# Stick-breaking queries and keys: one whole copy out of PSUM on ScalarE, then hi and lo from SBUF

## The chip, the cores and the metric

The kernel runs on one core of a Trainium2 chip. The metric is device time in microseconds (us): the median of three runs of the kernel before is 1643.02 us (1641.83 to 1644.89). The engines are called as in the profile: PE (TensorE matmul), PEld (TensorE weight load), DVE (VectorE), ACT (ScalarE), POOL (GpSimd), SP (SyncE).

## The reference, cut to what matters

The reference runs three transformer layers (a convolution mixer, a pooling mixer, and a block with two attention branches and a feed-forward part) on 512 tokens of width 1024. The change lies in the third, in stick-breaking attention with 16 heads of width 64:

```python
z = jnp.einsum('bhtd,bhsd->bhts', qb, kb).astype(jnp.float32) * scale      # scale = 64 ** -0.5 = 0.125
log_1m_beta = jnp.where(mask, jax.nn.log_sigmoid(-z), 0.0)
after = lax.cumsum(log_1m_beta, axis=3, reverse=True) - log_1m_beta
log_a = jax.nn.log_sigmoid(z) + after
a = jnp.where(mask, jnp.exp(log_a), 0.0)
outs.append(jnp.einsum('bhts,bhsd->bhtd', a.astype(v.dtype), vb))
```

q, k and v come from one projection of the normed input. Nothing of the mathematics is changed.

## The kernel before, in words

Matmuls run on fp32r numbers. To keep fp32 precision every operand is held as hi (the value rounded to fp32r) and lo (the value less hi), and a product is three matmuls, hi*hi, hi*lo and lo*hi. Weights arrive as fp32 blocks of 128x1024; `group_steps` makes their hi on ACT (L304) and their lo on DVE (L309).

Activations are kept transposed: 128 features on the partitions, 512 tokens in the free dimension. One 128x512 result of a q or k projection (`lin_in`, lines L320 to L322 with the three products) therefore holds two heads, one in partitions 0 to 63 and one in 64 to 127 (`HALF`). It is made in an accumulator `m`, of which there are two in PSUM (`psm`, bufs=2). All of these share the two `m` accumulators in turn: the q and k projections, the v projection (L1037 to L1039), and the output of a head (`sb_out`, L1185). A new user of an accumulator waits until the last reader of the one before has finished.

For a query pair i, `sb_q` makes two tiles of 128x512, one a head: one half holds hi and the other half lo of the same 64 rows. ACT writes the two hi halves from PSUM (L1084, with the factor 0.125), and one tick later DVE writes the two lo halves, reading PSUM again and hi from SBUF (L1087). For a key pair `sb_k` does the like: hi by ACT (L1094), lo by DVE into separate zeroed tiles (L1097), and a second copy of hi into the other half by ACT (L1099).

The stage walks over 16 heads. For head `hd` the steps are W (`sb_weights`: matmuls of the cumulative sums into the score banks z, L1161 and L1164; then ACT takes their exponentials, L1170), O (`sb_out` of the head before, L1185), S (`sb_scores` of the head after next, L1126 to L1134, into z banks that the exponentials just read), and three F (`fill`: half a q or k projection or one block of a v projection, taken in the order of `SB_ORDER`). S also posts the softplus of its scores: a minimum on DVE (L1141), Exp and Ln on ACT (L1142, L1143), a maximum on DVE (L1146), sums on POOL (L1150), hi on DVE (L1109) or ACT (L1107) and lo on POOL (L1110). Work on ACT, DVE and POOL is posted as tasks, and `tick` after each step lets a task go on when its delay of `WAIT` steps is over. The stage is scheduled by hand: each of the engines PE, ACT, DVE and POOL runs its instructions in the order in which the program writes them.

Four heads take two q, two k and one v projection, so the pattern repeats every four heads. Such a stretch is called a round below: the second one goes from about 558 to 617 us. The tag "s" is a ring of 14 buffers of 128x512 that score, softplus and weight tiles of the stage use in turn.

Of the kernel before, what the change touches and what calls it, by code (L numbers as in the profile page):

```python
# [12 lines left out]
ALU = mybir.AluOpType  # L13
# [123 lines left out]
def body(ctx: ExitStack, tc, ap, out):  # L137
# [12 lines left out]
    def nm(p):  # L150
        uid[0] += 1
        return f"{p}{uid[0]}"
# [18 lines left out]
    def at(tag="a", dt=F32, n=T):  # L171
        return phase[0].pool[tag].tile([P, n], dt, tag=tag, name=nm(tag))
# [16 lines left out]
    def f(x):  # L189
        return x.bitcast(F32)  # L190

    mm = nc.tensor.matmul
    V, A, G = nc.vector, nc.scalar, nc.gpsimd
# [8 lines left out]
    with tc.high_priority(offset=20000):  # L202
        for k in range(KC // 2):
            t = const.tile([P, 2 * T], F32, name=nm("x"))
# [124 lines left out]
    def acc():  # L329
        turn[0] += 1  # L330
        return pm() if turn[0] % 2 else pz()
# [491 lines left out]
    with tc.manual_schedule(engines=HAND):  # L823
# [8 lines left out]
        for k in range(KC):  # L832
            t = at("c")
# [36 lines left out]
        raw, zs = {}, [None] * KC  # L870
# [37 lines left out]
    for i in range(4):  # L908
        t = at("v" if i < 2 else "p")
# [117 lines left out]
    def sb_lin(w):  # L1027
        i = int(w[1:])
        if w[0] == "v":

            v_[i] = [at("a", F32R) for _ in range(4)]
            for j in range(4):
                o = pm()
                for k in range(KC):
                    wh, wl = block(2 * k, 2)
                    hh, hl = cols(h[k], j * P, j * P + P)
                    mm(o[:, 0:2 * P], hh, wh, start=k == 0, stop=False)  # L1037
                    mm(o[:, 0:2 * P], hh, wl, start=False, stop=False)
                    mm(o[:, 0:2 * P], hl, wh, start=False, stop=k == KC - 1)  # L1039
                post(split_steps(o[:, 0:2 * P].rearrange("p (h d) -> p h d", h=4), v_[i][j].rearrange("p (h s d) -> p h s d", h=4, s=2)))  # L1040
                if j == 3:
                    at_block[0] += 2 * KC
                yield
            return
        o = yield from lin_in((SBQ if w[0] == "q" else SBK) + i)
        ready[w] = post((sb_q if w[0] == "q" else sb_k)(i, o))
        yield
# [32 lines left out]
    def sb_q(i, o):  # L1080

        q_[i] = [at("a", F32R) for _ in HALF]
        for t, a in zip(q_[i], HALF):
            A.mul(out=t[a], in_=o[a], mul=0.125)  # L1084
        yield WAIT["q"]
        for t, a, b in zip(q_[i], HALF, HALF[::-1]):
            V.scalar_tensor_tensor(out=t[b], in0=o[a], scalar=0.125, in1=f(t[a]), op0=ALU.mult, op1=ALU.subtract)  # L1087

    def sb_k(i, o):

        res, los = [at("a", F32R) for _ in HALF], klo[i % 3]
        k_[i] = res, los
        for t, a in zip(res, HALF):
            A.copy(out=t[a], in_=o[a])  # L1094
        yield WAIT["k"]
        for t, lo, a in zip(res, los, HALF):
            V.tensor_sub(out=lo[a], in0=o[a], in1=f(t[a]))  # L1097
        for t, a, b in zip(res, HALF, HALF[::-1]):
            A.copy(out=t[b], in_=f(t[a]))  # L1099

# [120 lines left out]
    def fill_all():  # L1221
        for w, o in zip(SB_ORDER, first):
            finish(post((sb_q if w[0] == "q" else sb_k)(int(w[1:]), o)))
        for w in SB_ORDER[len(first):]:
            yield from sb_lin(w)
        yield from ret_qk(0)
        for e in range(4):
            o = yield from lin_in(RG + e)
            gate0.append(at("g"))
            V.tensor_copy(out=gate0[-1], in_=o)  # L1230
            yield
# [232 lines left out]
    with tc.manual_schedule(engines=HAND):  # L1464
# [5 lines left out]
        for a in (0, T // 2):  # L1470
            b = a + T // 2
            o = acc()
# [99 lines left out]
```

## Time and profile before

| what | value |
| --- | --- |
| median of three runs | 1643.02 us |
| the profiled execution | 1643.24 us, its span 1641.5 us |
| PE, PEld | 97%, 82% busy |
| DVE, ACT, POOL | 60%, 38%, 33% busy |
| attention stage, 455 to 710 us: PE, DVE, ACT, POOL | 243.9, 182.4, 157.8, 170.1 us busy of 255 |
| granted TensorE clock in that stage | 1.00 |

The profile is of one execution; its time is 1.7 us above its span, which goes from the first instruction to the last. Busy time of PE includes modelled ends of matmuls, so a wait of PE is best read from the waits and from starts in the order of time. A wait is written as idle time before an instruction, with the instruction that ended it.

### The profile page before, as it was taken

The page shows a single profiled execution, that of the slowest core. Times are in us where ns is not written, and L with a number is a line of the kernel's source. Part 1 is how long each engine was busy: PE and PEld are TensorE (multiplying, and loading weights), DVE is VectorE, ACT ScalarE, POOL GpSimd, SP SyncE. Part 2 cuts the span into 40 slices and gives each one's busy share as a digit, 9 for nine tenths or more (in the row PEclk, how much of TensorE's full clock was granted, in tenths as well). Part 3 has the DMA queues.
Part 4 walks back from the last instruction along what each step waited for, and adds up shares of the span by engine and source line. Part 5 has one row for each costly group of instructions (what it writes and reads, how often), then busy time and mean ns, then how long its engine had stood idle before and what let it go on. Part 6 is the DMA issues. An engine that isn't in the chain of part 4 may idle for free.

```text
span 1641.5 us, 20357 instructions
## 1 busy us (share of the span) xinstructions
PE 1584.5 (97%) x7910; PEld 1338.7 (82%) x7910; DVE 986.2 (60%) x1374; ACT 617.1 (38%) x918; POOL 541.4 (33%) x414
## 2 busy tenths in 40 slices
PE   7999899999999999999999999999999999999997
PEld 5788778877887888878878888888888888888887
DVE  7899988797777676874665744433255433333222
ACT  4634434433467656522323222123234322222221
POOL 2567853671256676720210202004522000000001
PEclk8999999999999999999999999999999999999998
DMA  9565444455422111245374321322222232223231
GB/s 347 172 214 184 143 141 148 149 175 196 161 63 67 52 52 52 78 147 165 105 235 144 109 90 54 120 78 90 93 95 75 97 103 93 100 95 99 91 101 52
DMA packets 61059, 197.97 MB, mean 121 GB/s; under 512 B 6689, under 2 KB 8993, under 8 KB 60962
## 3 DMA queue, kind: packets, MB, share of 16 engines
q1 hardware_dynamic: 58978, 193.52, 35.6%
q10 hardware_dynamic: 1984, 3.15, 0.6%
q8 instruction: 62, 1.02, 0.3%
q14 instruction: 35, 0.29, 0.1%
HBM read 194.54 MB, written 2.10 MB: 120 GB/s over the span
## 4 chain that ended last, share of the span: by engine, by line
PE 77%; DVE 10%; ACT 5%; issue 3%; DMA 2%; POOL 2%; SPq 0%; POOLq 0%; DVEq 0%; ACTq 0%
PE m L320 10%; PE m L322 10%; PE m L321 10%; PE z L322 8%; PE z L320 8%; PE z L321 8%; DVE wlo L309 3%; DVE gw L265 1%; DMA gw<-in_wmod 1%; PE m L1293 1%; PE z L1293 1%; PE z L1292 1%; PE m L1292 1%; PE m L1291 1%; PE z L1291 1%
## 5 line engine op out<-in xcount | busy, mean ns | idle before, releaser
L309 DVE TENSOR_TENSOR wlo<-w,whi 128x1024 fp32r<-128x1024 f32 (+1 forms) x244 | 334.0, 1372 | 359.3 <-ACT whi L304 358.8
L304 ACT CAST whi<-w 128x1024 fp32r<-128x1024 f32 x244 | 255.6, 1051 | 591.0 <-PE m L321 254.2
L320 PE MATMUL m<-h,whi 128*128 128x512 f32 x730 | 286.3, 392 | 2.5 <-DVE c L677 1.3
L321 PE MATMUL m<-h,whi 128*128 128x512 f32 x730 | 284.6, 390 | 2.0 <-POOL h L556 2.0
L322 PE MATMUL m<-h,wlo 128*128 128x512 f32 x730 | 285.1, 391 | 1.2 <-DVE wlo L309 1.2
L320 PEld LDWEIGHTS m<-h,whi 128*128 128x128 f32 x730 | 137.2, 188 | 31.3 <-DVE a L1087 1.7
L322 PEld LDWEIGHTS m<-h,wlo 128*128 128x128 f32 x730 | 137.1, 188 | 31.0 <-DVE wlo L309 2.0
L321 PEld LDWEIGHTS m<-h,whi 128*128 128x128 f32 x730 | 137.3, 188 | 29.9 <-POOL h L556 2.3
L410 POOL TENSOR_TENSOR c<-c,c 128x512 f32<-128x512 f32 x10 | 13.4, 1339 | 370.3 <-ACT c L448 370.1
L322 PE MATMUL z<-h,wlo 128*128 128x512 f32 x338 | 132.0, 391 | 0.2 <-DVE e L918 0.2
L320 PE MATMUL z<-h,whi 128*128 128x512 f32 x338 | 132.1, 391 | 0.0
L321 PE MATMUL z<-h,whi 128*128 128x512 f32 x338 | 131.8, 390 | 0.0
L410 POOL TENSOR_TENSOR s<-s,s 128x512 f32<-128x512 f32 x14 | 18.7, 1337 | 321.0 <-ACT s L1331 292.2
L1110 POOL TENSOR_TENSOR s<-s,s 128x512 fp32r<-128x512 f32 x64 | 96.1, 1514 | 12.7 <-DVE s L1109 12.7
L265 DVE CUSTOM_DVE_ANT_0 gw<-gw,cb,vec 128x1024 f32<-128x1024 f32 x59 | 90.1, 1535 | 5.0 <-DMA gw<-in_wmod 4.9
L322 PE MATMUL z<-a,wlo 128*128 128x512 f32 (+1 forms) x222 | 81.8, 368 | 1.5 <-DVE wlo L309 1.5
L320 PE MATMUL z<-a,whi 128*128 128x512 f32 (+1 forms) x222 | 82.1, 370 | 0.0
L321 PE MATMUL z<-a,whi 128*128 128x512 f32 (+1 forms) x222 | 81.5, 367 | 0.0
L322 PEld LDWEIGHTS z<-h,wlo 128*128 128x128 f32 x338 | 63.7, 188 | 14.3 <-DVE e L918 0.6
L321 PEld LDWEIGHTS z<-h,whi 128*128 128x128 f32 x338 | 63.7, 188 | 13.0
L320 PEld LDWEIGHTS z<-h,whi 128*128 128x128 f32 x338 | 63.7, 189 | 12.9
L320 PE MATMUL m<-a,whi 128*128 128x512 f32 (+1 forms) x196 | 71.5, 365 | 0.0
(430 smaller groups left out, 3527.7 us busy)
## 6 DMA issues: line engine op xcount, KB each, us to landing
w<-in_weights SPq DMA_DIRECT2D x244, 512.0 KB, 3.7
gw<-in_wmod SPq DMA_DIRECT2D x86, 512.0 KB, 4.3
a<-in_diag SPq DMA_DIRECT2D x40, 256.0 KB, 5.2
dg<-in_wmod SPq DMA_DIRECT2D x10, 256.0 KB, 7.0
y<-in_wmod SPq DMA_DIRECT2D x10, 256.0 KB, 5.8
x<-in_xt SPq DMA_DIRECT2D x4, 512.0 KB, 6.0
s<-in_dec ACTq DMA_DIRECT2D x4, 256.0 KB, 3.3
out_x<-h SPq DMA_DIRECT2D x4, 256.0 KB, 2.5
```

Of the source, the lines that this page charges most:

```text
L265: product = V.tensor_tensor_reduce(out=t, in0=t, in1=cb[-1][:, a:b], scale=1.0, scalar=mod[:, j:j + 1] if a else bias_of(j), op0=ALU.mult, ...
L304: A.copy(out=hi, in_=w)
L309: e.tensor_tensor(out=lo[:, part], in0=w[:, part], in1=f(hi[:, part]), op=ALU.subtract)
L320: mm(o, l[0], r[0], start=first, stop=False)
L321: mm(o, l[0], r[1], start=False, stop=False)
L322: mm(o, l[1], r[0], start=False, stop=last)
L410: self.eng.tensor_tensor(out=n, in0=self.acc, in1=t, op=ALU.add)
L1110: G.tensor_tensor(out=lo[:, 0:w], in0=t[:, 0:w], in1=f(hi[:, 0:w]), op=ALU.subtract)
L1291: mm(o, hh, wh, start=k == 0, stop=False)
L1292: mm(o, hh, wl, start=False, stop=False)
L1293: mm(o, hl, wh, start=False, stop=k == KC - 1)
```

## The change

`sb_q` and `sb_k` take one new tile each from the ring "s". ACT writes the whole 128x512 accumulator into it in one operation (with the factor for q, a copy for k). The hi halves are then made by ACT from this tile, and the lo halves by DVE, which subtracts hi from it; for q the DVE operation is a plain subtraction now. PSUM is read by the first operation alone.

```diff
     def sb_q(i, o):
 
         q_[i] = [at("a", F32R) for _ in HALF]
+        raw = at("s")
+        A.mul(out=raw, in_=o, mul=0.125)
         for t, a in zip(q_[i], HALF):
-            A.mul(out=t[a], in_=o[a], mul=0.125)
+            A.copy(out=t[a], in_=raw[a])
         yield WAIT["q"]
         for t, a, b in zip(q_[i], HALF, HALF[::-1]):
-            V.scalar_tensor_tensor(out=t[b], in0=o[a], scalar=0.125, in1=f(t[a]), op0=ALU.mult, op1=ALU.subtract)
+            V.tensor_sub(out=t[b], in0=raw[a], in1=f(t[a]))
 
     def sb_k(i, o):
 
         res, los = [at("a", F32R) for _ in HALF], klo[i % 3]
         k_[i] = res, los
+        raw = at("s")
+        A.copy(out=raw, in_=o)
         for t, a in zip(res, HALF):
-            A.copy(out=t[a], in_=o[a])
+            A.copy(out=t[a], in_=raw[a])
         yield WAIT["k"]
         for t, lo, a in zip(res, los, HALF):
-            V.tensor_sub(out=lo[a], in0=o[a], in1=f(t[a]))
+            V.tensor_sub(out=lo[a], in0=raw[a], in1=f(t[a]))
         for t, a, b in zip(res, HALF, HALF[::-1]):
             A.copy(out=t[b], in_=f(t[a]))
```

The new line numbers are L1084 and L1086 (q on ACT), L1089 (q on DVE), L1096, L1098 and L1103 (k on ACT), L1101 (k on DVE); every line behind them is four higher than before (L1174 for L1170, L1189 for L1185).

On ACT, before, the second key of the second round (accumulator m_5543), the weights' hi, one v block and the exponentials of the head whose z banks the next scores take:

```order
L1094 CAST a_5583<-m_5543 64x512
L1094 CAST a_5584<-m_5543 64x512
L1099 CAST a_5583<-a_5583 64x512
L1099 CAST a_5584<-a_5584 64x512
L304 CAST whi_5604<-w_5544 128x1024
L1076 CAST a_5597<-m_5601 128x4x64
L1170 ACTIVATE s_5646<-z_5368 128x512
L1170 ACTIVATE u_5647<-r_5369 128x256
L1170 ACTIVATE s_5648<-z_5370 128x512
```

The same place of ACT after the change:

```order
L1096 COPY s_5607<-m_5565 128x512
L1098 CAST a_5605<-s_5607 64x512
L1098 CAST a_5606<-s_5607 64x512
L1103 CAST a_5605<-a_5605 64x512
L1103 CAST a_5606<-a_5606 64x512
L304 CAST whi_5628<-w_5566 128x1024
L1076 CAST a_5621<-m_5625 128x4x64
L1174 ACTIVATE s_5670<-z_5386 128x512
L1174 ACTIVATE u_5671<-r_5387 128x256
L1174 ACTIVATE s_5672<-z_5388 128x512
```

One row is new, ahead of the two hi casts, which read it; nothing else has moved, and the exponentials stand behind all of it.

On DVE, before, the second query of the second round (accumulator m_5430), between the maxima and the casts of the softplus:

```order
L1146 TENSOR_TENSOR s_5384<-z_5370,s_5384 128x512
L1087 SCALAR_TENSOR_TENSOR a_5467<-m_5430,a_5467 64x512
L1087 SCALAR_TENSOR_TENSOR a_5468<-m_5430,a_5468 64x512
L1109 CAST u_5491<-u_5383 128x256
L1109 CAST s_5495<-s_5382 128x512
```

The same place of DVE after the change:

```order
L1150 TENSOR_TENSOR s_5402<-z_5388,s_5402 128x512
L1089 TENSOR_TENSOR a_5487<-s_5489,a_5487 64x512
L1089 TENSOR_TENSOR a_5488<-s_5489,a_5488 64x512
L1113 CAST u_5513<-u_5401 128x256
L1113 CAST s_5517<-s_5400 128x512
```

The count and the order of DVE's instructions stay; the two of the query read s_5489 and hi, both in SBUF, where they read the accumulator and hi. PE's order does not change.

## Rows read from the trace of the kernel before

**Rows 1.** Waits of PE, 455 to 710 us: total us, times, longest.
```profile
PE m L1185 <- DVE g L1097: 5.0, 3, 1.7
PE m L1185 <- DVE a L1087: 3.5, 3, 1.5
```

**Rows 2.** Busy us (instructions) by stretch: PE, PEld, DVE, ACT, POOL; clock, DMA.
```profile
562.54:569.33 6.79, 6.79 (x33) 5.71 (x32) 1.38 (x2) 6.61 (x11) 2.74 (x3) 1.00 0.00 0
569.36:580.05 10.69, 10.26 (x54) 8.50 (x53) 10.49 (x14) 5.01 (x9) 7.44 (x7) 1.00 0.17 52
580.08:588.30 8.22, 6.36 (x42) 5.52 (x41) 5.69 (x10) 8.02 (x15) 4.56 (x6) 1.00 0.19 64
675.00:710.00 35.00, 35.00 (x174) 29.84 (x173) 28.52 (x39) 16.09 (x29) 26.23 (x21) 1.00 0.20 69
```

**Rows 3.** ACT in order of time, second round: start, us, instruction, idle before.
```profile
562.54 1.18 ACT L1094 CAST a<-m 64x512 fp32r<-64x512 f32 x2 [3.02 <-PE m L322]
...
569.36 1.20 ACT L1084 ACTIVATE a<-m 64x512 fp32r<-64x512 f32 x2
...
580.08 0.63 ACT L1142 ACTIVATE s<-s 128x512 f32<-128x512 f32 x1 [5.63 <-DVE s L1141]
...
583.23 1.17 ACT L1094 CAST a<-m 64x512 fp32r<-64x512 f32 x2
584.31 1.25 ACT L1099 CAST a<-a 64x512 fp32r<-64x512 f32 x2
...
587.68 0.62 ACT L1170 ACTIVATE s<-z 128x512 f32<-128x512 f32 x1
```

**Rows 4.** DVE in order of time, second round.
```profile
569.36 1.23 DVE L309 TENSOR_TENSOR wlo<-w,whi 128x1024 fp32r<-128x1024 f32 x1 [4.22 <-ACT whi L304]
...
572.27 1.39 DVE L1087 SCALAR_TENSOR_TENSOR a<-m,a 64x512 fp32r<-64x512 f32 x2
...
577.02 2.31 DVE L309 TENSOR_TENSOR wlo<-w,whi 128x1024 fp32r<-128x1024 f32 x1
...
589.54 0.74 DVE L1109 CAST s<-s 128x512 fp32r<-128x512 f32 x2
```

**Rows 5.** PE in order of time, second round.
```profile
583.96 0.34 PE L1164 MATMUL z<-s,cstr 128*128 128x384 f32 x1
585.97 1.05 PE L1185 MATMUL m<-s,a 128*128 128x512 f32 x4 [1.67 <-DVE g L1097]
...
588.35 0.50 PE L1126 MATMUL z<-a,a 128*128 128x512 f32 x1
```

**Rows 6.** ACT by line and shape, whole span: count, busy us, mean ns, idle before.
```profile
L1351 ACT COPY a<-m 128x512 f32<-128x512 f32 x4 | 2.3, 576 | 0.0
```

**Rows 7.** PE in order of time, first query of the second round.
```profile
556.60 1.06 PE L1185 MATMUL m<-s,a 128*128 128x512 f32 x4 [1.48 <-DVE a L1087]
...
558.37 0.39 PE L1126 MATMUL z<-a,a 128*128 128x512 f32 x1
```

**Rows 8.** ACT in order of time, the same place.
```profile
553.85 1.18 ACT L1084 ACTIVATE a<-m 64x512 fp32r<-64x512 f32 x2
...
556.88 0.61 ACT L1170 ACTIVATE s<-z 128x512 f32<-128x512 f32 x1
```

**Rows 9.** DVE in order of time, start of the stage.
```profile
475.92 0.42 DVE L1078 TENSOR_TENSOR a<-m,a 128x256 fp32r<-128x256 f32 x1
```

**Rows 10.** PE in order of time, start of the stage.
```profile
476.91 0.28 PE L1037 MATMUL m<-whi,h 128*128 128x256 f32 x1
```

**Rows 11.** POOL in order of time, second round.
```profile
542.05 1.29 POOL L1110 TENSOR_TENSOR s<-s,s 128x512 fp32r<-128x512 f32 x1
...
572.32 0.74 POOL L1150 TENSOR_TENSOR s<-s,u 128x256 f32<-128x256 f32 x1
...
576.90 3.57 POOL L1110 TENSOR_TENSOR s<-s,s 128x512 fp32r<-128x512 f32 x2 [0.43 <-DVE s L1109]
...
589.44 2.00 POOL L1110 TENSOR_TENSOR s<-s,s 128x512 fp32r<-128x512 f32 x1
```

**Rows 12.** DVE by line and shape, 455 to 715 us.
```profile
L393 DVE TENSOR_TENSOR a<-s,a 128x512 fp32r<-128x512 f32 x4 | 2.8, 693 | 0.1
```

## The prediction

> **What bounds the kernel now.** Read the waits of PE in the attention stage first [rows 1]. The reader is to see that PE, busy nearly all the time, waits six times for an accumulator `m` that DVE has not yet finished reading, 5.0 us behind L1097 and 3.5 us behind L1087: 8.5 us in all, and the change frees `m` much sooner, after one ACT operation. That is the gain on offer. It is not yet a gain in time: the question is what PE would wait for next.
>
> So read PE around one of these waits [rows 5]. The last L1164 of step W starts at 583.96 and O (L1185) follows at 585.97, after 1.67 us for DVE's L1097. Then comes S, whose last score matmul (L1126) starts at 588.35. ACT's last exponential of the z bank that it overwrites runs from 587.68 to 588.30 [rows 3]. PE followed it by 0.05 us. The wait for `m` thus ended just before another one: behind it stands ACT.
>
> Now follow ACT and DVE back from 588.30. ACT started this run of work at 580.08, released by DVE's L1141 after 5.63 us idle [rows 3], and was busy 8.02 of the 8.22 us since [rows 2]. DVE started its run at 569.36, released by ACT's weight cast L304 after 4.22 us idle [rows 4], and was busy 10.49 of 10.69 us until L1141's end at 580.05 [rows 2]. ACT started that run at 562.54 with the key cast L1094, released by PE after 3.02 us idle [rows 3], and was busy 6.61 of 6.79 us until the weight cast's end at 569.33 [rows 2]. (The missing 0.2 us in each are the steps from one instruction to the next.) From 562.54 to 588.35 there is one unbroken chain, ACT, DVE, ACT, and then PE. It holds both keys of the round: L1094 at 562.54 and at 583.23 [rows 3]. A share of busy time would not show it: ACT is at 38% over the span.
>
> **The change part by part.**
>
> ACT, added: one 128x512 operation from PSUM for each of 8 queries and 8 keys. A copy of this form takes 0.58 us [rows 6], an activation from PSUM 0.61 [rows 8]. The hi casts can't start before it has ended; a hand-over between dependent instructions is 0.03 us here (DVE's L1141 ends at 580.05, ACT starts at 580.08) [rows 2, 3]. The two hi casts stay, with an SBUF source: two such casts take 1.25 us (L1099) [rows 3]. For a key: 0.58 + 0.03 + 1.25 = 1.86 us in place of 1.18 [rows 3], +0.68. For a query: 0.61 + 0.03 + 1.25 = 1.89 in place of 1.20 [rows 3], +0.69; I count 0.68 for both, and only those on the chain.
>
> Round: two keys on it, 2 x 0.68 = +1.36 us for S at 588.35. The second query's casts (569.36) [rows 3] stand behind the weight cast from which DVE goes on, so they are not on it. The 1.67 us for `m` go: the copy would end at 583.23 + 0.68 + 0.58 = 584.49, and PE comes to O later than before by what has already been lost. O comes early, and PE waits at S for the exponentials. There are three rounds: +4.08 us.
>
> First query of each round: PE's O waited 1.48 us for L1087, until 556.60, and S's last matmul came at 558.37 [rows 7]. ACT's last exponential ended at 556.88 + 0.61 = 557.49 [rows 8]. It ends 0.68 later now, at 558.17, PE follows at 558.22, so of the wait removed only 0.15 us is kept. Three times: -0.45 us.
>
> Start of the stage: query 0 and key 0 are cast one behind the other ahead of the weight casts, and key 1 stands on the same way to the first v blocks: 3 x 0.68 = 2.04 us on the way to DVE's L1078, which ends at 476.34 [rows 9] and frees the accumulator that PE takes at 476.91 [rows 10]. Of it 0.57 us is slack: +1.47 us.
>
> DVE: the 32 lo subtractions. From PSUM and SBUF two take 1.39 us, 0.69 each [rows 4]; a subtraction with both inputs in SBUF takes 0.69 us where it runs alone [rows 12]. So the operation costs the same, and a gain is excluded by that row. But the place of its inputs counts: the weights' lo (L309, both inputs in SBUF) takes 1.23 us at 569.36 and 2.31 at 577.02 [rows 4], where POOL's L1110 had begun at 576.90; there two L1110 take 3.57 us [rows 11], where one alone takes 1.29 [rows 11]. Each waited for the other. It can fall to DVE too: at 589.54 two casts take 0.74 us [rows 4] and it is POOL's L1110 of 589.44 that takes 2.00 [rows 11]. The second query's pair (572.27) is on the chain, with POOL's L1150 of 0.74 us beginning at 572.32 [rows 11]. Its cost is between 0 (DVE keeps its turn) and 0.74 us (the second subtraction waits for the whole L1150). The two rows speak for one end each, so I take the middle, 0.35 to 0.37, say 0.35 us a round: +1.05 us. The keys' pairs lie beside ACT's work: DVE has 4.22 us idle after the first [rows 4].
>
> The Trainium skill says on this, in "SBUF — State Buffer", section "Who interferes with whom", that a VectorE instruction with two SBUF inputs contends with a GpSimd one that reads SBUF, and that whichever issues second is blocked until the first is done. The trace agrees with the blocking (2.31 against 1.23 us). By that rule L1150 issues ahead of the second subtraction and the term would be 3 x 0.74 = 2.2 us in place of 1.05, the time 1650.3.
>
> Ring "s": the new tile waits for POOL in most cases. For the first query of the second round the built program gives it the buffer that POOL's L1110 of 542.05 read last, free at 543.34 [rows 11]; the cast stands at 553.85 [rows 8]. Cost nothing, hidden by 10 us. No DMA is added or moved.
>
> Sum: 4.08 - 0.45 + 1.47 + 1.05 = 6.15 us, on the profiled execution's 1643.24 us (span 1641.5 and 1.7 us around it) 1649.4; the median of runs stands 0.2 us below, so **1649.2 us**. Nothing gives it back after the last key: from 675 to 710 us PE is busy 35.00 of 35.00 us [rows 2], and what follows starts from PE.
>
> **The rivals.**
>
> Faster: the accumulator waits are what counts, and PE is through O and S earlier. All 8.5 us of rows 1 go: 1643.0 - 8.5 = 1634.5. For it: PE is the engine that is busy, and these waits are its longest. Against it: the exponential that ends 0.05 us ahead of the last score matmul. It decides if the chain through ACT has slack of 0.68 us or more between key and exponential; its busy shares leave 0.2.
>
> No change: DVE's chain catches up. L309 at 577.02 lost 2.31 - 1.23 = 1.08 us to POOL; if DVE comes later and meets a free POOL, a round gets 1.08 back: 6.15 - 3.24 = 2.9, 1645.9. Against it: that L1110 was released by DVE's own L1109 (0.43 us idle before it) [rows 11], so it moves along.
>
> Slower still: every subtraction of the second query waits for POOL, once 0.74 (L1150) and once 1.29 us (L1110), 2.03 a round in place of 0.35: 6.15 + 5.04 = 11.2, 1654.2. It decides if POOL has an instruction under way when each subtraction is issued. POOL is busy 7.44 of 10.69 us there [rows 2], but only the L1150 are close by.
>
> **How the numbers follow.** What a measurement can tell from no change here is about 0.2%, 3.3 us. The forecast has 0.58, with its own range 1648 to 1651 (the middle term at 0 gives 1648.1, at 0.74 1650.3, and 0.05 us on each of nine tasks 0.5 more). No change has 0.14, faster 0.07, slower still 0.21. Faster by over 0.2%: 0.07; within: 0.14; slower: 0.58 + 0.21 = 0.79. The range goes from 1645.0, which takes in the catching-up case at 1645.9, to 1653.0, where POOL costs most of its bound; left out are the faster case and the far end of the slower one, about 2 in 10.
>
> **What would show it.** In the profile after, PE waits for `m` behind DVE's subtractions should be gone, and L1130 (S) should wait for ACT's L1174 by 1 to 3 us a head in three of four heads, some 15 us in all (the 8.5 of the waits that go and the 6.15 lost). The key's three ACT operations should take 1.86 us, with the exponentials still ending 0.05 us before S. L1089 should read 0.69 us alone and up to 1.4 us beside L1154 on POOL. The prediction is wrong if ACT shows idle time between L1096 and L1174, or if S waits no more than before.

## The result, and the profile after

The changed kernel takes 1653.37 us (median of 4 runs, 1652.64 to 1653.78), the kernel before 1643.42 us in the same comparison; the ratio is 1.006 with a 95% interval of 1.0048 to 1.0072. It is 9.95 us slower. The forecast was +6.15 us, and its range ended at 1653.0. The profiled run took 1652.64 us, its span is 1650.9 us.

The waits of PE in the stage first, with the same columns as [rows 1]:

```profile
PE z L1130 <- ACT s L1174: 11.9, 9, 1.8
PE m L1037 <- DVE a L1078: 0.8, 1, 0.8
```

The 8.5 us behind DVE's subtractions are gone, and in their place stands S (L1130), waiting for the last exponentials of ACT nine times, at three heads of four. So far this is the forecast, though the sum is 11.9 us where it had some 15. The new thing is in the next view, the three rounds by stretch (busy us and instructions of PE, PEld, DVE, ACT, POOL, then the granted clock):

```profile
500.00:558.00 58.00, 54.61 (x303) 48.20 (x302) 38.58 (x60) 36.63 (x69) 39.51 (x35) 0.94 0.16 55
558.00:617.00 59.00, 54.61 (x303) 48.39 (x303) 40.23 (x60) 37.56 (x69) 40.00 (x35) 0.94 0.14 46
617.00:676.00 59.00, 54.60 (x305) 48.45 (x304) 39.34 (x60) 39.84 (x74) 38.39 (x35) 0.94 0.17 54
```

The clock is 0.94; before it was 1.00 in every stretch of [rows 2] and over the whole second round:

```profile
558.00:617.00 59.00, 55.17 (x322) 48.46 (x322) 40.64 (x63) 38.45 (x72) 39.79 (x37) 1.00 0.16 54
```

Cut finer in the second round of the changed kernel, after two of the waits at S:

```profile
576.00:578.00 2.00, 1.59 (x8) 1.35 (x9) 1.94 (x4) 1.95 (x6) 1.69 (x2) 0.92 0.76 256
578.00:580.00 2.00, 2.00 (x7) 1.71 (x7) 1.94 (x4) 1.53 (x3) 1.73 (x2) 0.50 0.05 14
...
594.00:596.00 2.00, 1.91 (x10) 1.68 (x9) 1.95 (x6) 1.64 (x4) 1.44 (x2) 0.68 0.50 129
596.00:598.00 2.00, 2.00 (x10) 1.90 (x10) 1.74 (x4) 0.00 (x0) 2.00 (x2) 0.50 0.33 133
598.00:600.00 2.00, 2.00 (x19) 2.00 (x17) 0.00 (x0) 0.00 (x0) 2.00 (x3) 0.96 0.00 0
```

At 0.50 the clock is at its lower level, 1.2 GHz: from 596 to 598 us PE is busy all the time and does 10 matmuls, where it does 19, nearly all of the same size, in the next 2 us. This happens six times in the stage, twice a round, each time behind the wait at the second or the third S of the round, and each time 1.7 us of clock are lost (the sum of one less the granted clock over short stretches). The Trainium skill says in "TensorE: Matmul & The Clock Gate", section "What's actually happening", that the array's clock follows how busy PE has been and has two levels; the rows agree with that much.

Now PE in order of time, second round: the last score matmul of each S (128x512), and around the third S the end of O and the wait:

```profile
562.11 0.50 PE L1130 MATMUL z<-a,a 128*128 128x512 f32 x1
...
577.09 0.50 PE L1130 MATMUL z<-a,a 128*128 128x512 f32 x1
...
591.37 0.33 PE L1189 MATMUL m<-s,a 128*128 128x128 f32 x2
593.52 0.51 PE L1130 MATMUL z<-a,a 128*128 128x384 f32 x2 [1.81 <-ACT s L1174]
...
594.28 0.50 PE L1130 MATMUL z<-a,a 128*128 128x512 f32 x1
...
609.41 0.39 PE L1130 MATMUL z<-a,a 128*128 128x512 f32 x1
...
623.94 0.51 PE L1130 MATMUL z<-a,a 128*128 128x512 f32 x1
```

From one S to the next this gives four intervals, A to D, in each round: 577.09 - 562.11 = 14.98, then 17.19, 15.13 and 14.53 us. The S at 577.09 is called the second S of the round below, and the one at 594.28 the third. The kernel before starts the same matmuls at 558.37 [rows 7], 588.35 [rows 5] and

```profile
572.00 0.50 PE L1126 MATMUL z<-a,a 128*128 128x512 f32 x1
...
601.96 0.39 PE L1126 MATMUL z<-a,a 128*128 128x512 f32 x1
...
616.75 0.39 PE L1126 MATMUL z<-a,a 128*128 128x512 f32 x1
```

which gives 13.63, 16.35, 13.61, 14.79. A round is 3.45 us longer: A +1.35, B +0.84, C +1.52, D -0.26. The forecast for a round was 1.36 + 0.35 - 0.15 = 1.56, all of it in A, B and D. A and B are read together, since A also holds the copy of the second query, which stands ahead of the exponentials of the second S, and B gives that back (in e11 below, where the pair does not meet POOL, A is 14.84 and B 16.35 as before): +2.19 where 1.71 was forecast. C is new: the matmuls that run at half the clock from 594 on are in it.

ACT in the same place, answering to [rows 3]:

```profile
585.32 0.63 ACT L1146 ACTIVATE s<-s 128x512 f32<-128x512 f32 x1 [5.79 <-DVE s L1145]
...
588.46 0.58 ACT L1096 COPY s<-m 128x512 f32<-128x512 f32 x1
589.07 1.27 ACT L1098 CAST a<-s 64x512 fp32r<-64x512 f32 x2
590.36 1.26 ACT L1103 CAST a<-a 64x512 fp32r<-64x512 f32 x2
591.65 1.04 ACT L304 CAST whi<-w 128x1024 fp32r<-128x1024 f32 x1
...
593.62 0.61 ACT L1174 ACTIVATE s<-z 128x512 f32<-128x512 f32 x1
```

The key takes 588.46 to 590.34, 1.88 us (forecast 1.86). The last exponential ends at 594.23, and PE follows at 594.28, again 0.05 us later. And DVE, where the second query's pair meets POOL:

```profile
576.68 1.83 DVE L1089 TENSOR_TENSOR a<-s,a 64x512 fp32r<-64x512 f32 x2
578.54 1.00 DVE L1113 CAST u<-u 128x256 fp32r<-128x256 f32 x1
```

```profile
576.73 1.23 POOL L1154 TENSOR_TENSOR s<-s,u 128x256 f32<-128x256 f32 x1
578.04 1.35 POOL L1154 TENSOR_TENSOR s<-s,s 128x384 f32<-128x384 f32 x1
```

The pair takes 1.83 us, where the pair from PSUM took 1.39 [rows 4]; and POOL's L1154, which took 0.74 us [rows 11], takes 1.23. Both got longer at once. The Trainium skill says in "SBUF — State Buffer", section "Who interferes with whom", that a VectorE instruction with two SBUF inputs contends with a GpSimd one that reads SBUF; these rows agree.

### The profile page after: what moved, and what is told of

Same layout as the page of the kernel before. It is cut to its first block, busy times and chain, and to the rows that moved or that the text cites. A ratio compares the mean times of both kernels' runs of the same rounds, so it can differ in the third digit from the quotient of the medians.

```text
span 1650.9 us, 20374 instructions
## 1 busy us (share of the span) xinstructions
PE 1590.7 (96%) x7910; PEld 1344.0 (81%) x7910; DVE 991.4 (60%) x1374; ACT 626.5 (38%) x934; POOL 548.9 (33%) x414
## 4 chain that ended last, share of the span: by engine, by line
PE 79%; DVE 9%; ACT 5%; issue 2%; DMA 2%; POOL 1%; SPq 0%; POOLq 0%; DVEq 0%; ACTq 0%
PE m L320 11%; PE m L322 11%; PE m L321 11%; PE z L322 8%; PE z L320 8%; PE z L321 8%; DVE wlo L309 3%; DVE gw L265 1%; DMA dg<-in_wmod 1%; ACT whi L304 1%; PE m L1297 1%; PE z L1295 1%; PE m L1295 1%; PE z L1297 1%; PE m L1037 1%
## 5 line engine op out<-in xcount | busy, mean ns | idle before, releaser
L309 DVE TENSOR_TENSOR wlo<-w,whi 128x1024 fp32r<-128x1024 f32 (+1 forms) x244 | 334.3, 1373 | 359.3 <-ACT whi L304 358.8
```

Source lines behind the costliest of these rows:

```text
L309: e.tensor_tensor(out=lo[:, part], in0=w[:, part], in1=f(hi[:, part]), op=ALU.subtract)
```

## The experiments

Theory A: ACT's part of the chain costs 1:1 and moves PE's idle time to one place, S; the clock falls behind it, and that is what the forecast lacked. Theory B: the fallen clock fills time in which PE would wait anyway, and DVE and POOL are in each other's way more than forecast. All times are medians of 5 runs (e6, e8 and e10 of 11) against the kernel before on the same chip (1643.5, 1642.9 and 1643.0 us in the three comparisons; the changed kernel was measured against 1643.4). In brackets stand the ratio to the kernel before and its 95% interval. The intervals below are those of the second round, from starts of the last score matmul of S in the profiled run; the last column says how many of the three C intervals of the stage had a fallen clock.

| kernel | median us | A | B | C | D | C at half clock |
| --- | --- | --- | --- | --- | --- | --- |
| before | 1643.0 | 13.63 | 16.35 | 13.61 | 14.79 | 0 of 3 |
| changed | 1653.4 | 14.98 | 17.19 | 15.13 | 14.53 | 3 |
| e1 filler, second and third S | 1652.3 | 14.96 | 17.18 | 15.11 | 14.52 | 3 |
| e2 queries only | 1650.0 | 14.36 | 16.50 | 13.62 | 14.51 | 2 |
| e3 keys only | 1649.1 | 14.19 | 17.01 | 15.10 | 14.75 | 2 |
| e4 lo from PSUM | 1649.4 | 14.84 | 16.62 | 16.01 | 14.77 | 1 |
| e5 filler, third S | 1649.0 | 14.97 | 17.21 | 13.59 | 14.49 | 0 |
| e6 copies on DVE | 1644.1 | 13.59 | 15.90 | 13.62 | 14.54 | 2 |
| e7 before, copies on DVE | 1635.3 | 13.03 | 14.88 | 13.50 | 14.77 | 0 |
| e8 keys only, copies on DVE | 1641.2 | 13.07 | 15.51 | 15.11 | 14.78 | 3 |
| e9 before, extra ACT copy | 1649.5 | 14.19 | 16.93 | 14.95 | 14.75 | 1 |
| e10 as e6, filler at third S | 1640.5 | 13.55 | 15.91 | 13.64 | 14.47 | 0 |
| e11 query's lo from PSUM | 1650.6 | 14.84 | 16.35 | 15.04 | 14.77 | 2 |

### Filling the wait: e1 and e5

```diff
         o = pm()
+        for _ in range(4 if hd in (1, 2, 5, 6, 9, 10) else 0):
+            mm(o, v_[i // 2][0][:, hd % 4 * P:hd % 4 * P + P], aa[0][0], start=True, stop=True)
         for j in range(4):
```

> The changed kernel, and on PE four more 128x512 matmuls ahead of O (into the accumulator that O then starts anew) in the six heads whose S waited 1.5 to 2.0 us for ACT; they take about 0.9 us out of that wait and add nothing that is used. Theory A (the idle stretch at S lets the granted clock fall to half for some 3.4 us, and the slow matmuls behind it are what the prediction lacked): clock 1.00 over the stage, S's waits there down to 0.6 to 1.2 us, time 1649 to 1650.5. Theory B (the fallen clock fills time that PE would wait anyway; what was lacking is DVE and POOL in each other's way): the same time as the changed kernel, 1653.4, or up to 1 us more.

Measured 1652.3 us (1.0058, 1.0046 to 1.0071). The wait at the second S fell and the clock stayed there; the third S kept its wait and its fall:

```profile
PE z L1130 <- ACT s L1174: 9.8, 9, 2.0
```

Half of the expectation failed: three falls went, and the time hardly moved. The table says why. B is 17.18 us with the fall (changed) and without it (e1): behind the second S the slow matmuls only use up the wait that PE meets at the third S. C has no such wait at its end, and there the fall goes with 1.5 us. So the next run fills the third S alone.

```diff
+        for _ in range(12 if hd in (2, 6, 10) else 0):
+            mm(o, v_[i // 2][0][:, hd % 4 * P:hd % 4 * P + P], aa[0][0], start=True, stop=True)
```

> As the filler run, but twelve unused matmuls ahead of O in the three heads (at 527, 586 and 644 us of the kernel before) behind whose S PE lost 1.5 us each time that the clock fell, and none elsewhere; the wait at S there falls from 2.2 to about 0.5 us. Theory A' (a fallen clock costs time only where PE is not made to wait for ACT a head later; the three falls behind the other S are hidden by the next wait): these three falls go, the other three stay, and the time is 1653.4 - 3 x 1.5 = 1648.9. Theory B (the falls cost nothing; the loss is in the chain of ACT, DVE and POOL alone): 1652.3 to 1653.4.

Measured 1649.0 us (1.0038, 1.0024 to 1.0052), as theory A' has it. Its second and third rounds:

```profile
558.00:617.00 59.00, 56.02 (x322) 49.09 (x321) 41.32 (x62) 39.15 (x73) 40.08 (x35) 1.00 0.17 54
617.00:676.00 59.00, 55.98 (x324) 49.25 (x323) 41.41 (x61) 39.19 (x72) 41.76 (x36) 1.00 0.19 60
```

C is back at 13.59, A and B of this round are those of the changed kernel. Matmuls that compute nothing of use made the kernel 4.4 us faster than the changed one by the medians; in the profiled runs the three rounds, from the S of 500 us on, are 4.3 us shorter (166.58 against 170.85). (One fall was left, behind the second S of the first round, where the expectation had three. There B is 17.62 and not 17.2: with the wait at the third S filled, such a fall is no longer hidden whole.) Theory B falls in so far as it has the falls cost nothing; that DVE and POOL cost more than forecast is taken up with e4 and e11.

### One part alone: e2 and e3

Kernel e2 has the new `sb_q` and the old `sb_k`, e3 the other way round.

> Only the queries take the new tile; the keys are as before. Theory A: the three waits for m behind L1087 go (3.5 us), those behind L1097 stay (5.0 us); the second query's subtractions cost 0.70 us a round against POOL, the first query gives back 0.45 us in all, the start costs 0.1 us: 2.1 - 0.45 + 0.1 = +1.8, 1645.2, clock 1.00 in the stage. Theory B (contention is the larger part of the loss, about 2 us a round): 1649. If the ring or the order mattered apart from that: above 1649.

> Only the keys take the new tile; the queries are as before. Theory A: ACT's chain is 0.68 us longer for each of six keys, 4.1 us, and 0.8 us at the start: 1648.3 with the clock at 1.00; S waits for ACT at the same places, so the clock falls at some of them and the time is 1650 to 1652. Theory B (contention of the queries' subtractions is the larger part): 1647 to 1648.5, whatever the clock does.

The queries alone: 1650.0 us (1.0042, 1.0028 to 1.0056), 4.8 us over the expectation. Without a fallen clock the second round has A + B + C + D = 58.99, 0.61 over before. But PE's waits for `m` behind the key's subtractions have grown:

```profile
PE m L1187 <- DVE g L1099: 7.0, 3, 2.3
```

They were 5.0 us, 1.7 at most [rows 1]: the contention of the query's pair makes DVE late, the wait at O is longer, and behind it the clock fell in the first and the third round (in the third C is 16.05 us). In the second round the same wait (2.35 us) was not followed by a fall. So this run too has a part of clock that the expectation lacked. The keys alone: 1649.1 us (1.0034, 1.0020 to 1.0048), 0.9 us under the range that theory A gave with a falling clock; C is 15.12 and 15.10 where it fell and 13.60 where it did not. A + B is 31.20, +1.22 for the two keys where the forecast had 1.36.

### Contention: e4 and e11

```diff
-            V.tensor_sub(out=t[b], in0=raw[a], in1=f(t[a]))
+            V.scalar_tensor_tensor(out=t[b], in0=o[a], scalar=0.125, in1=f(t[a]), op0=ALU.mult, op1=ALU.subtract)
```

This is e11; e4 has besides `in0=o[a]` in the key's subtraction.

> ACT as in the changed kernel (whole copy, casts from it), but DVE's subtractions read the accumulator again, as before. This gives up the early release of m and takes away every conflict of these subtractions with POOL. Theory A: the waits for m come back, each 0.7 us later than in the kernel before, so that the idle time is split between O and S and the clock stays at 1.00; 4.1 (keys) + 1.5 (start) + 2.0 (first query of three rounds) = +7.6, 1650.6. Theory B (contention is the larger part of the loss): 1648 or less, since that is gone.

> The changed kernel, but the queries' subtractions read the accumulator and not the new tile (three operations on ACT as in the changed kernel). Theory A: the second query's pair and the cast behind it no longer meet POOL, which gives 0.70 us a round between the S of 558 and of 588 us (a shift of 1.4 us in place of 2.2 there); the waits for m behind L1087 come back and cost 0.25 to 0.7 us a round at the first query; the clock falls as in the changed kernel: 1651.5 to 1653. If contention cost nothing: a shift of 2.2 us there as before, and 1654.

Measured 1649.4 us (1.0038, 1.0025 to 1.0051) and 1650.6 us (1.0042, 1.0029 to 1.0055). The subtractions of e11 by shape, count, busy us and mean ns:

```profile
L1089 DVE SCALAR_TENSOR_TENSOR a<-m,a 64x512 fp32r<-64x512 f32 x14 | 9.6, 689 | 1.7 <-ACT a L1086 1.3
```

From PSUM the 14 take 683 to 694 ns, 689 on average; from the new tile the 16 take 889 on average. A + B is 31.20 to 31.23 in the three rounds of e11 and 31.27 to 31.45 in e4, against 32.12 to 32.17 with contention: 0.7 to 1.0 us a round, not the 0.35 of the forecast and not the 2.03 of the rival. In the medians both runs missed: e4 lies between its two theories, and e11 0.9 us under its range, with falls behind the third S in two rounds of three. In e4 the clock was forecast to stay. It fell behind the third S in one round of three and stayed down twice as long as in the changed kernel (C is 16.01 us), and once behind the second S, so that idle time in two pieces keeps the clock is not borne out.

### ACT alone: e9

```diff
             A.copy(out=t[b], in_=f(t[a]))
+        A.copy(out=at("s"), in_=f(res[1]))
```

> The kernel before with one unused 128x512 copy on ACT behind the second hi copies of each key (about 0.6 us), from SBUF to a tile of ring s; queries, accumulators and DVE's subtractions as before. Theory A (ACT's work in that chain costs 1:1): 0.6 x 2 x 3 = 3.6 us and about 1.2 us at the start, 1647.9 with the clock at 1.00; the wait at the third S grows to about 1 us, and where the clock falls behind it 0.8 to 2.4 us each are added: 1648 to 1651. Theory C (the change costs through what it does to PSUM, to m and to the subtractions, not through ACT's time): 1643 to 1644.

Measured 1649.5 us (1.0036, 1.0023 to 1.0050): the kernel before with 0.6 us more of ACT for a key, and nothing else changed. A + B is 31.12 against 29.98, +1.14 for two keys. In the second round the clock fell, C is 14.95. So ACT's time on the chain alone, without the new reading of SBUF and without the early release of `m`, makes the kernel 6.5 us slower, and theory C falls.

### Taking work off ACT: e6, e7, e8, e10

```diff
-            A.copy(out=t[b], in_=f(t[a]))
+            V.tensor_copy(out=t[b], in_=f(t[a]))
```

> The changed kernel with the second hi copies of the keys (L1103, 1.25 us of ACT for a key) moved to DVE (about 0.84 us for two, most of it in DVE's idle time ahead of the weights' lo). Theory A (ACT's part of the chain sets S, 1:1): a key then costs 0.68 - 1.25 = -0.57 us of ACT against the kernel before; 2 x 1.25 x 3 = 7.5 us less than the changed kernel, and with the waits at S under 1.2 us the clock stays at 1.00, another 4.5 us: 1640 to 1642. If DVE is the tighter engine: 1648 to 1653.

> The kernel before with the same move of the second hi copies (L1099) to DVE, without the new tile. Theory A: the first key of a round gives 1.25 us to the chain, the second only to S, behind a wait for m that stays: 3 x 1.25 = 3.75 us, 1639 to 1640; PE still waits for m behind L1097 and L1087. If the waits for m alone set the time of the kernel before: 1643.

> Keys with the new tile and their second copies on DVE; queries as in the kernel before, so that the query's subtractions do not meet POOL. Theory A: against the run with both parts and copies on DVE it saves 0.70 us a round of contention and brings back the waits for m behind L1087 (1.5 us a round, of which 0.15 counts): 1639 to 1641.

Measured: e6 1644.1 us (1.0007, 0.9998 to 1.0016), e7 1635.3 us (0.9953, 0.9940 to 0.9965), e8 1641.2 us (0.9993, 0.9984 to 1.0002). e6 and e8 stand above their ranges, with falls in C in two and three rounds. e7 beats both kernels, by 7.6 us, more than expected: a round is 2.2 us shorter (56.18 against 58.38), not 1.25. The second key's copies count too: S stood behind the exponentials [rows 3, 5], not behind O alone. Its ACT, where [rows 3] had the second copies (1.25 us) between the casts and what follows:

```profile
579.07 1.16 ACT L1094 CAST a<-m 64x512 fp32r<-64x512 f32 x2
580.25 1.05 ACT L304 CAST whi<-w 128x1024 fp32r<-128x1024 f32 x1
```

```profile
PE m L1185 <- DVE g L1097: 4.4, 3, 1.5
PE m L1185 <- DVE a L1087: 3.4, 3, 1.5
```

The waits for `m` are nearly all still there, 7.8 us of 8.5, and the kernel is faster than any other run here. So the 7.6 us did not need them gone; what bound the kernel before was ACT's work on the chain.

For e6 one more run fills the third S, with eight matmuls in place of twelve:

> The changed kernel with the keys' second copies on DVE, and eight unused matmuls ahead of O in the three heads whose S still waited 1.9 us for ACT. Theory A' (what that kernel lacked against its forecast is the fallen clock at these three places): clock 1.00 from 520 to 676 us and 1639.5 to 1641. Without a part of the clock in it: 1644.

Measured 1640.5 us (0.9987, 0.9978 to 0.9996), 3.6 us under e6:

```profile
558.00:617.00 59.00, 57.60 (x333) 50.72 (x333) 45.89 (x70) 38.37 (x72) 42.49 (x38) 1.00 0.19 58
```

What e6 lacked against its forecast was the clock again: C is 15.02 and 16.08 in the rounds of e6 where it fell, and 13.6 in all three of e10. Even so, with its waits filled, the changed kernel stays 5.2 us behind e7, which has the same copies on DVE and no new tile.

## Why the prediction was wrong

**The bound and the chain** were read rightly. The waits for `m` went, S took their place, PE started 0.05 us behind the exponentials, and the key's operations took 1.88 us. e9 shows the price of ACT's time by itself.

**The step that failed** is "O comes early, and PE waits at S for the exponentials". The wait was priced by the lateness of ACT alone, as if PE went on behind it at its old speed; a fall of the clock was put at nothing. Before, PE idled 1.67 us ahead of O [rows 5] and 0.15 us ahead of S, between the last matmuls of O and the first of S:

```profile
587.10 0.33 PE L1185 MATMUL m<-s,a 128*128 128x128 f32 x2
587.58 0.50 PE L1126 MATMUL z<-a,a 128*128 128x384 f32 x2
```

Now the idle time is one wait of 1.8 us at S. Behind it the clock fell in all three rounds, and in C, where no further wait takes the loss up, that costs 1.5 us a round. Three rounds make 4.5 us; e5 fills the waits and takes 4.3 to 4.4 us out. Why the clock fell behind these waits and not behind those at O is not shown: a wait of 1.33 us at the second S was followed by a fall in each round of the changed kernel, and none of the five waits of 1.5 to 1.7 us at O before was (527 to 645 us; [rows 5, 7] show two).

**The contention term** was mis-sized: 0.35 us a round was the middle between 0 and 0.74; e4 and e11 give 0.7 to 1.0. By the upper end the forecast without the clock is 1650.3, which with 4.5 us for the clock would be 1654.8.

**The sum, term by term.** In the profiled runs the changed kernel is 10.48 us slower from the S of 500 to that of 660 us (170.85 against 160.37), and 1.27 us before that, from the first S of the stage on: 11.75 in all. C, forecast at 0, has 4.5 us of it. A and B have 6.5 where 5.1 were forecast: the keys cost a little less (1.2 us a round for 1.36), contention about 0.6 more. The first query's term, -0.15 a round, measured as -0.26 (D), and the start is within 0.1 us of its forecast.

**The forecast of 1649.2** is near e5 at 1649.0, which has the whole change and the contention in it but hardly a fallen clock in the stage. That it is so near is partly luck: the contention that was forecast too small and scatter outside the stage cancel.

**The rivals.** "Slower still" has nearly the right time, 1654.2, by the wrong mechanism. "No change" assumed that DVE catches up by meeting a free POOL: the second L309 of the round took 2.31 us as before, and DVE lost more to POOL at the query's pair. "Faster" took the waits for `m` as the bound; they went, and the kernel was slower.

**Outside the stage's heads** the change does nothing, and yet the spans differ by 9.4 us (1650.9 and 1641.5), 2.35 less than the 11.75 within. This is scatter: what lies ahead of the first query cast and behind the S of about 660 us takes 1438.6 us in the profile of before and 1436.2 in that of after, and 1435.9 to 1438.6 in those of the eleven experiments, none of which changes anything there.

## What to carry to other kernels

Freeing a buffer earlier is worth only what its waiter would do next: look for the wait that ends just behind the one that goes, and see whether the cure lengthens it. When PE's idle time moves to another place, price a fall of the clock behind it as well as the wait, give it a chance of its own, and ask whether a later wait takes that loss up. Where ACT is on the chain, taking an operation off it (here two copies a key to an engine that was idle there) gained 7.6 us, and taking away the waits that looked longest gained nothing by itself.

## What the runs showed of the hardware

The clock fell to 0.50 behind waits of PE at the second and the third S in the changed kernel (1.3 to 1.8 us), all six times, and behind none of the third S's whose waits were filled in e5 and e10. The length of the wait alone does not decide it. Waits of 1.4 to 1.5 us at the third S of e8 were followed by a fall in all three rounds; waits of 1.4 to 1.7 us at O, in the kernel before and in e7, ten in all, by none.

```profile
PE z L1128 <- ACT s L1172: 4.9, 4, 1.5
```

That is e8; e7's waits at O are shown above. The same wait in one kernel can have either end: 1.35 us at the second S of e5 came before a fall in one round of three, 2.7 us at the third S of e3 in two of three, 2.3 us at O in e2 in two of three. The runs do not show what decides it.

A subtraction on DVE with both inputs in SBUF and an instruction of POOL lengthen each other (0.74 to 1.23 us on POOL, 1.39 to 1.83 us for the pair, 0.60 to 1.00 us for the cast behind it), where the same subtraction from PSUM took 683 to 694 ns every time in e11.
